# RMS norms at four stage boundaries: all eight blocks' squares summed by TensorE, and a weight split tied to the last residual

## The chip, the cores and the metric

The kernel runs on one core of one Trainium2 chip. The core's engines work from queues of their own: TensorE (PE; its weight loads are shown apart as PEld) multiplies matrices, VectorE (DVE) and ScalarE (ACT) do elementwise work, GpSimd (POOL) does next to nothing here, SyncE (SP) issues the transfers (DMAs). Each engine executes its own instructions strictly in the order in which they were recorded, and waits where an operand is not ready. The metric is the time of one execution in microseconds (us); of several runs the median is taken.

## The reference

The model is two blocks in a row on 256 tokens of width 1024, everything in float32. The first block has two layers, each a mixer (attention, short convolution, pooling) and a product-key expert layer ("peer"); the second block has another mixer, cross-attention and a gated feed-forward layer. Between the stages stands an RMS norm over the width of 1024:

```python
def rms_norm(t, g):
    tf = t.astype(jnp.float32)
    y = tf * lax.rsqrt(jnp.mean(tf * tf, axis=-1, keepdims=True) + EPS)
    return (y * g.astype(jnp.float32)).astype(t.dtype)

for l in range(DEPTH):                     # DEPTH = 2
    ...
    h = rms_norm(x, norm1_g[l]) * (1.0 + scale1) + shift1
    z = h @ w_in[l]
    ...
    x = x + gate1 * mix                    # mixer residual
    h2 = rms_norm(x, norm2_g[l]) * (1.0 + scale2) + shift2
    x = x + gate2 * peer_ffn(h2, peer_wq[l], ...)   # peer residual
# then the second block: h = rmsnorm(x, mix_norm_w); proj = h @ w_in_2; ...
```

## The kernel before

The activation `x` lies transposed in on-chip memory: eight blocks of 128 channels (partitions) by 256 tokens, `x[:, b]`. A float32 product is made from three products of rounded parts: every weight block of 128x1024 is loaded into a buffer `raw` (four of them), split by ScalarE into a high part `whi` (L509) and by VectorE into the rest `wlo` (L510), and multiplied by TensorE with the high and low parts `h` of the activation (L590, L591, L594; in the first two weight blocks behind a norm, whose matmuls are interleaved, L578, L579 and L582, below called the lead).

The method `norm` is called at four places, called boundaries here: from the first mixer to the first peer layer, from there to the second mixer, from there to the second peer layer, and from there to the mixer of the second block. It goes through these steps:

1. `warm(warm[0])`: 8 (before a peer layer) or 16 (before a mixer) warm-up matmuls (L546, a 128x512 product of the table `iota`, its result is read by nobody). `warm[1]` (6 or 8) and `warm[2]` (2 or 4) more follow below.
2. `rms_sums`: ScalarE squares each block into a tile `sq` (L471, out of a ring of four tiles of 128x256), as soon as that block's residual has been added (`use_out`, L894, in a mixer; `residual`, L1224, in a peer layer). For six blocks VectorE adds the squares up one after the other (L473); then TensorE multiplies that sum, and the squares of the last two blocks, with a column of ones (L465), two matmuls of one output column for each, and so adds over the channels into a tile of the PSUM pool C.
3. The split of the first weights behind the norm, tied by `issue_after(self.last_v)` to stand on VectorE behind the instruction that `last_v` names: the last of the five additions.
4. `rms_end`: mean and inverse root on VectorE (L479, L441 to L445), then TensorE spreads the row over the partitions (`rms_row`, L502), the second weights are split, and VectorE and ScalarE make `t`, `h` high and `h` low (L553, L561, L568) for the lead.

The order in each queue is made when the program is built: a scheduler places the instructions by their dependences and its own estimate of time, keeping to the order that `issue_after` asks for. So warm-up matmuls written behind the sums may land ahead of some of them. Other places of the program that sum squares (cross-attention, L1613, where TensorE takes all eight blocks; the feed-forward layer, L1675) do not go through `norm`.

Of the kernel before, what the change touches and what calls it, by code (L numbers as in the profile page):

```python
# [15 lines left out]
ALU = mybir.AluOpType  # L16
# [6 lines left out]
KB = 8  # L23
# [205 lines left out]
class Kernel:  # L229
# [287 lines left out]
    def norm(self, src, A, B=None, warm=WB):  # L517

        self.warm(warm[0])
        after = lambda: self.tc.issue_after(self.last_v)  # L520
        ss = self.rms_sums(src, KB)
        with after():
            a = self.split_w(self.next[0])
        with after():
            cols = self.rms_end(ss, D)
        self.warm(warm[1])
        row = self.rms_row(cols)
        self.warm(warm[2])
        with after():
            self.next = [a, self.split_w(self.next[1])]  # L530
        last = self.last_v
        pair = self.act_pair(self.wp, "h")
        t = {}
        for i in range(KB):
            with self.tc.issue_after(last):
                t[i] = self.norm_scale(src, A, row, i)
            self.norm_hi(pair, t[i], B, i)
        for i in range(KB):
            self.norm_lo(pair, t[i], B, i)
        return pair  # L540
# [153 lines left out]
    def mixer(self, l):  # L694
        nc, V, S, tc = self.nc, self.nc.vector, self.nc.scalar, self.tc
        with tc.tile_pool(name=f"att{l}", bufs=1) as ap:
# [194 lines left out]
            gate = self.mod[l][:, 16:24]  # L891

            def use_out(nb, ps):
                V.scalar_tensor_tensor(self.x[:, nb], ps, gate[:, nb:nb + 1], self.x[:, nb],  # L894
                                       op0=ALU.mult, op1=ALU.add)

            self.proj(self.a[f"wout{l}"], range(KB), (mhi, mlo), use_out,
                      kbs=[(k, k) for k in (4, 5, 6, 7, 0, 1, 2, 3)], each=each)
            each(99)
# [202 lines left out]
    def peer(self, l, keep, nxt, late=None):  # L1102
        nc, V, S, tc = self.nc, self.nc.vector, self.nc.scalar, self.tc
# [14 lines left out]
        with ExitStack() as st:  # L1118
# [69 lines left out]
            for i in range(NPEER):  # L1188
                vh, vl = self.split_w(self.raw(self.a[f"v{l}"][:, i]))
                src = gb[i // 64][:, i % 64]  # L1190
# [22 lines left out]
            gate = self.mod[l][:, 40:48]  # L1213
# [6 lines left out]
            def residual(b):  # L1220
                pt = self.pC([P, T])
                for t in range(2):
                    nc.tensor.transpose(pt[:, t * P:(t + 1) * P], yn[t][:, b * P:(b + 1) * P], self.ident)
                V.scalar_tensor_tensor(self.x[:, b], pt, gate[:, b:b + 1], self.x[:, b], op0=ALU.mult, op1=ALU.add)  # L1224

            for w in held:
                down(w, [0])
# [2 lines left out]
            for t in range(2):  # L1230
                residual(2 * t)
                residual(2 * t + 1)
                down(held[1], [1], [t])
            evacuate(1)
            for b in range(4, KB):
                residual(b)
# [544 lines left out]
```

## Time and profile before

| what | value |
|---|---|
| median of 3 runs | 2333.07 us (2330.46 to 2334.24) |
| the profiled execution, its whole time | 2334.84 us |
| its span (first to last instruction) | 2333.0 us |
| TensorE busy | 2297.4 us, 98% of the span |
| VectorE busy | 1904.7 us, 82% |
| ScalarE busy | 1208.7 us, 52% |
| mean granted clock of TensorE | 0.995 of full speed |
| share of TensorE in the chain that ended last | 91% (VectorE 5%, DMA 2%, ScalarE 1%) |

The span is what the rows further down divide up; 1.84 us of the execution lie outside it. The chain that ended last is followed back from the last instruction through what released each step; TensorE's share there says how much of the time is its own work. A line like "L546 A<-iota x8" is a group of like instructions of source line 546 that write a tile of the PSUM pool A from the tile `iota`. A matmul of float32 operands shows as two records in the trace, called passes below, so the two matmuls of one block's squares are four passes.

### The profile page before, as it was taken

How to read it: one execution, taken by the hardware profiler on the slowest of the kernel's cores; microseconds unless marked ns; L12 is line 12 of the kernel's file. 1: busy time of each engine (PE TensorE's matmuls, PEld its weight loads, DVE VectorE, ACT ScalarE, POOL GpSimd, SP SyncE). 2: the span in 40 equal slices, each digit the busy share in tenths (PEclk: the TensorE clock that was granted, in tenths of full speed). 3: DMA queues.
4: the chain of work that ended last, by engine and by line, in shares of the span. 5: the costliest groups of instructions: out<-in, count | busy, mean ns of one | idle time of the engine just before them, and what ended most of it. 6: DMA issues, size and time to landing. Idle time of an engine off the chain costs nothing.

```text
span 2333.0 us, 42534 instructions
## 1 busy us (share of the span) xinstructions
PE 2297.4 (98%) x16209; PEld 2046.3 (88%) x16209; DVE 1904.7 (82%) x4205; ACT 1208.7 (52%) x1884; POOL 4.8 (0%) x20
## 2 busy tenths in 40 slices
PE   8999999999999999999999999999999999999998
PEld 7989999988888878888999988888878878999997
DVE  6884999788899985576599888888888879767766
ACT  4474445555544455565454555554456654556553
POOL 0000000000000000000000000000000000000000
PEclk9999999999999999999999999999999999999999
DMA  8874556555677786544566655555556652345652
GB/s 300 284 259 156 200 198 214 177 171 172 224 228 235 256 297 201 175 141 130 172 207 200 204 173 171 171 173 176 172 183 193 193 181 84 123 165 189 194 187 82
DMA packets 124781, 443.96 MB, mean 190 GB/s; under 512 B 14240, under 2 KB 17440, under 8 KB 123808
## 3 DMA queue, kind: packets, MB, share of 16 engines
q1 hardware_dynamic: 124576, 441.24, 57.2%
q8 instruction: 127, 2.08, 0.4%
q14 instruction: 78, 0.64, 0.1%
HBM read 437.26 MB, written 3.93 MB: 189 GB/s over the span
## 4 chain that ended last, share of the span: by engine, by line
PE 91%; DVE 5%; DMA 2%; ACT 1%; issue 1%; SPq 0%; DVEq 0%; ACTq 0%
PE A L1183 29%; PE B L1140 10%; PE B L590 10%; PE B L591 10%; PE B L594 10%; PE B L1143 5%; PE A L1685 2%; PE C L1095 1%; PE C L1096 1%; DVE wlo L510 1%; PE C L594 1%; PE C L591 1%; PE C L590 1%; DMA adas<-in_wada 1%; PE A L935 1%
## 5 line engine op out<-in xcount | busy, mean ns | idle before, releaser
L510 DVE TENSOR_TENSOR wlo<-raw,whi 128x1024 fp32r<-128x1024 f32 (+1 forms) x715 | 849.0, 1189 | 249.2 <-issue 105.1
L509 ACT ACTIVATE whi<-raw 128x1024 fp32r<-128x1024 f32 (+1 forms) x715 | 735.7, 1032 | 219.0 <-PE B L594 126.9
L590 PE MATMUL B<-h,whi 128*128 128x256 f32 x2080 | 518.8, 286 | 0.6 <-ACT zs L1487 0.6
L591 PE MATMUL B<-h,whi 128*128 128x256 f32 x2080 | 515.7, 284 | 0.0
L590 PEld LDWEIGHTS B<-h,whi 128*128 128x128 f32 x2080 | 397.5, 191 | 3.5 <-ACT zs L1487 1.3
L591 PEld LDWEIGHTS B<-h,whi 128*128 128x128 f32 x2080 | 397.7, 191 | 2.3 <-issue 1.5
L1183 PE MATMUL A<-whi,ah 128*128 128x512 f32 x1024 | 323.1, 395 | 0.0
L1183 PE MATMUL A<-wlo,ah 128*128 128x512 f32 x1024 | 319.0, 392 | 2.4 <-DVE wlo L510 2.3
L1183 PE MATMUL A<-whi,al 128*128 128x512 f32 x1024 | 316.7, 389 | 0.0
L594 PE MATMUL B<-h,wlo 128*128 128x256 f32 x2080 | 293.9, 283 | 0.0
L509 ACT ACTIVATE ah<-gb 128x256 fp32r<-128x256 f32 x256 | 106.6, 417 | 323.1 <-PE A L1183 316.0
L594 PEld LDWEIGHTS B<-h,wlo 128*128 128x128 f32 x2080 | 268.5, 191 | 0.5 <-issue 0.3
L1140 PE MATMUL B<-h,whi 128*128 128x512 f32 x1024 | 260.8, 397 | 0.0
L1183 PEld LDWEIGHTS A<-wlo,ah 128*128 128x128 f32 x1024 | 191.7, 188 | 45.3 <-DVE wlo L510 5.1
L1183 PEld LDWEIGHTS A<-whi,al 128*128 128x128 f32 x1024 | 192.2, 188 | 41.9 <-DVE al L510 0.2
L1183 PEld LDWEIGHTS A<-whi,ah 128*128 128x128 f32 x1024 | 187.5, 188 | 34.9
L1140 PEld LDWEIGHTS B<-h,whi 128*128 128x128 f32 x1024 | 183.6, 189 | 32.2
L1143 PEld LDWEIGHTS B<-h,wlo 128*128 128x128 f32 x1024 | 139.7, 190 | 10.0
L1146 ACT ACTIVATE gb<-B 128x256 f32<-128x256 f32 x128 | 49.3, 385 | 187.5 <-PE B L1143 187.5
L1143 PE MATMUL B<-h,wlo 128*128 128x256 f32 x1024 | 142.5, 282 | 0.0
L510 DVE TENSOR_TENSOR al<-gb,ah 128x256 fp32r<-128x256 f32 x256 | 106.9, 417 | 0.0
L1130 ACT ACTIVATE gb<-B 128x512 f32<-128x512 f32 x64 | 38.4, 600 | 106.8 <-PE B L594 106.8
(483 smaller groups left out, 2805.1 us busy)
## 6 DMA issues: line engine op xcount, KB each, us to landing
raw<-in_u SPq DMA_DIRECT2D x256, 512.0 KB, 3.3
raw<-in_v SPq DMA_DIRECT2D x256, 512.0 KB, 4.2
raw<-in_win SPq DMA_DIRECT2D x50, 512.0 KB, 3.7
raw<-in_ffn SPq DMA_DIRECT2D x44, 512.0 KB, 4.2
adaw<-in_wada SPq DMA_DIRECT2D x40, 512.0 KB, 4.9
adas<-in_wada SPq DMA_DIRECT2D x40, 512.0 KB, 4.9
raw<-in_wq SPq DMA_DIRECT2D x32, 512.0 KB, 3.4
raw<-in_wout SPq DMA_DIRECT2D x24, 512.0 KB, 3.5
```

What stands on the lines that cost most here:

```text
L509: self.nc.scalar.activation(hi[s], src[s], AF.Copy)
L510: self.last_v = self.nc.vector.tensor_sub(lo[s], src[s], hi[s].bitcast(F32)).ins
L590: self.nc.tensor.matmul(ps, wh[:, s], xh[:, kx], start=first and i == 0, stop=False)
L591: self.nc.tensor.matmul(ps, wh[:, s], xl[:, kx], start=False, stop=False)
L594: self.nc.tensor.matmul(ps, wl[:, s], xh[:, kx], start=False, stop=last and i == n - 1)
L935: nc.tensor.matmul(sp[:, t, half], qs[2 * hd + half][:, t * P:(t + 1) * P], keys[:, half], start=True, stop=True)
L1130: S.activation(gb[i // 32][:, 2 * i:2 * i + 2], ps, AF.Gelu)
L1140: nc.tensor.matmul(ps, wh[:, k * P:(k + 1) * P], both[:, :, k], start=k == 0, stop=False, skip_group_check=True)
L1143: nc.tensor.matmul(ps[:, 0], wl[:, k * P:(k + 1) * P], h[0][:, k], start=False, stop=k == KB - 1, skip_group_check=True)
L1146: S.activation(gb[1][:, j + e], ps[:, 1], AF.Copy)
L1183: nc.tensor.matmul(y[t][c], a_[:, s], v_[:, c * 512:(c + 1) * 512], start=(i == 0 and n == 0), stop=(i == NPEER - 1 and n == 2), skip_grou ...
L1685: nc.tensor.matmul(y[t][c], x_[:, s], w_[:, c * 512:(c + 1) * 512], start=False, stop=j == FF - 1 and n == 2, skip_group_check=True)
```

## The change

`norm` asks `rms_sums` for all eight blocks on TensorE. With that the loop of additions has no block left, the sums go to a tile of the PSUM pool B instead of C (as `rms_sums` does wherever more than two blocks go to TensorE), and TensorE gets eight pairs of one-column matmuls at each boundary where it had three. Both residuals now note themselves in `last_v`; since no addition sets `last_v` any more, the split of the first weights is tied to stand behind the last residual.

```diff
@@ norm
-        ss = self.rms_sums(src, KB)
+        ss = self.rms_sums(src, KB, KB)
@@ mixer, use_out
-                V.scalar_tensor_tensor(self.x[:, nb], ps, gate[:, nb:nb + 1], self.x[:, nb],
-                                       op0=ALU.mult, op1=ALU.add)
+                self.last_v = V.scalar_tensor_tensor(self.x[:, nb], ps, gate[:, nb:nb + 1], self.x[:, nb],
+                                                     op0=ALU.mult, op1=ALU.add).ins
@@ peer, residual
-                V.scalar_tensor_tensor(self.x[:, b], pt, gate[:, b:b + 1], self.x[:, b], op0=ALU.mult, op1=ALU.add)
+                self.last_v = V.scalar_tensor_tensor(self.x[:, b], pt, gate[:, b:b + 1], self.x[:, b], op0=ALU.mult,
+                                                     op1=ALU.add).ins
```

First place: TensorE at the first boundary, from the last product of the first mixer (L594) to the row's spreading (L502). Before, eight warm-up matmuls stand ahead of the sums (the first of them is shown) and six behind (A_2138), then two more (A_2148):

```order
L594 MATMUL B_2044<-h_867,wlo_2041 128x256 x8
L414 MATMUL C_2075<-c1t,part_1853 128x1
L546 LDWEIGHTS iota
L546 MATMUL A_2083<-iota 128x512
...
L465 MATMUL C_2109<-c1t,sq_2106 128x1 x2
L465 MATMUL C_2109<-c1t,sq_2112 128x1 x2
L465 MATMUL C_2109<-c1t,sq_2116 128x1 x2
...
L546 MATMUL A_2138<-iota 128x512
...
L546 MATMUL A_2148<-iota 128x512
L502 MATMUL C_2145<-c1t,rs_2126 128x128 x2
```

And now; the same eight stand ahead, and the six of A_2143 stand two behind sq_2105, two behind sq_2109, one behind sq_2113 and one behind sq_2117 (only the first is shown):

```order
L546 MATMUL A_2083<-iota 128x512
...
L465 MATMUL B_2092<-c1t,sq_2093 128x1 x2
L465 MATMUL B_2092<-c1t,sq_2097 128x1 x2
L465 MATMUL B_2092<-c1t,sq_2101 128x1 x2
L465 MATMUL B_2092<-c1t,sq_2105 128x1 x2
...
L546 MATMUL A_2143<-iota 128x512
L465 MATMUL B_2092<-c1t,sq_2109 128x1 x2
...
L465 MATMUL B_2092<-c1t,sq_2113 128x1 x2
...
L465 MATMUL B_2092<-c1t,sq_2117 128x1 x2
...
L465 MATMUL B_2092<-c1t,sq_2121 128x1 x2
...
L546 MATMUL A_2153<-iota 128x512
...
L502 MATMUL C_2150<-c1t,rs_2131 128x128 x2
```

Five pairs of sums are new, and six warm-up matmuls moved from behind the sums to among them; the third boundary has the same order.

Second place: VectorE at the first boundary, from the residual of the sixth block to the mean (`ms`); `sq` are the squares, `wlo_2121` and `wlo_2126` the low part of the first weights. Before:

```order
L894 SCALAR_TENSOR_TENSOR x<-B_1972,mod_68,x 128x256
L421 TENSOR_TENSOR mod_68<-mod_68,vt 128x1
L473 TENSOR_TENSOR sq_2094<-sq_2094,sq_2092 128x256
...
L473 TENSOR_TENSOR sq_2106<-sq_2106,sq_2103 128x256
L894 SCALAR_TENSOR_TENSOR x<-B_2008,mod_68,x 128x256
L510 TENSOR_TENSOR wlo_2121<-raw_2079,whi_2120 128x1024
L894 SCALAR_TENSOR_TENSOR x<-B_2044,mod_68,x 128x256
L415 TENSOR_TENSOR mod_68<-C_2075,vt 128x1
L951 COPY nat_2206<-iota 128x16
L433 SCALAR_TENSOR_TENSOR Acol<-mod_68,vt 128x8
L479 TENSOR_SCALAR ms_2124<-C_2109 128x2
```

And now:

```order
L894 SCALAR_TENSOR_TENSOR x<-B_1972,mod_68,x 128x256
L421 TENSOR_TENSOR mod_68<-mod_68,vt 128x1
L894 SCALAR_TENSOR_TENSOR x<-B_2008,mod_68,x 128x256
L894 SCALAR_TENSOR_TENSOR x<-B_2044,mod_68,x 128x256
L415 TENSOR_TENSOR mod_68<-C_2075,vt 128x1
L510 TENSOR_TENSOR wlo_2126<-raw_2079,whi_2125 128x1024
L433 SCALAR_TENSOR_TENSOR Acol<-mod_68,vt 128x8
L951 COPY nat_2211<-iota 128x16
L955 CAST first_2213<-fd_2214 128x16
L479 TENSOR_SCALAR ms_2129<-B_2092 128x2
```

The five additions are gone and the split moved from ahead of the last residual to behind it.

Third place: TensorE at the second boundary, from the first transposes of the peer layer's upper half (L1223, `yn` is the layer's result) to the sums. Before, the warm-up matmuls of A_11552 stand 1, 4, 4, 1 and 6 in the gaps:

```order
L1223 MATMUL C_11517<-c1t,yn_11471 128x128
...
L1223 MATMUL C_11521<-c1t,yn_11471 128x128
...
L1223 MATMUL C_11517<-c1t,yn_11472 128x128
L1223 MATMUL C_11521<-c1t,yn_11472 128x128
...
L1223 MATMUL C_11525<-c1t,yn_11471 128x128
L1223 MATMUL C_11525<-c1t,yn_11472 128x128
...
L1223 MATMUL C_11529<-c1t,yn_11471 128x128
L1223 MATMUL C_11529<-c1t,yn_11472 128x128
...
L546 MATMUL A_11552<-iota 128x512
L465 MATMUL C_11586<-c1t,sq_11583 128x1 x2
```

And now 1, 2, 3, 1 and 9 (A_11557):

```order
L1223 MATMUL C_11522<-c1t,yn_11476 128x128
...
L1223 MATMUL C_11526<-c1t,yn_11476 128x128
...
L1223 MATMUL C_11522<-c1t,yn_11477 128x128
L1223 MATMUL C_11526<-c1t,yn_11477 128x128
...
L1223 MATMUL C_11530<-c1t,yn_11476 128x128
L1223 MATMUL C_11530<-c1t,yn_11477 128x128
...
L1223 MATMUL C_11534<-c1t,yn_11476 128x128
L1223 MATMUL C_11534<-c1t,yn_11477 128x128
...
L546 MATMUL A_11557<-iota 128x512
L465 MATMUL B_11574<-c1t,sq_11575 128x1 x2
```

Three warm-up matmuls moved from ahead of the last transposes to behind them; the sums that follow have six more among them (2, 2, 1, 1) as at the first boundary, and the fourth boundary has the order of the second. On SyncE one load of the peer layer's query weights (the fifth block) moved behind the loads of `keys`, `first` and `crow`, at the first and the third boundary.

## Rows read from the trace of the kernel before

**Rows 1.** The page: busy time of each engine, share of the span, instructions

```profile
PE 2297.4 (98%) x16209; PEld 2046.3 (88%) x16209; DVE 1904.7 (82%) x4205; ACT 1208.7 (52%) x1884; POOL 4.8 (0%) x20
```

**Rows 2.** Windows: stretch, its length, busy us by engine, TensorE clock, DMA

```profile
1200.00:1900.00 700.00, 699.20 (x4718) 609.37 (x4717) 607.13 (x1327) 370.58 (x532) 0.00 (x0) 1.00 0.57 184
```

**Rows 3.** Timeline, TensorE, first boundary: start, us, what, idle before and releaser

```profile
173.96 1.89 PE L546 MATMUL A<-iota 128*128 128x512 f16 x8
175.69 1.40 PE L465 MATMUL C<-c1t,sq 128*128 128x1 f32 x12
176.94 1.89 PE L546 MATMUL A<-iota 128*128 128x512 f16 x8
179.30 0.71 PE L502 MATMUL C<-c1t,rs 128*128 128x128 f32 x4 [0.47 <-DVE rs L445]
181.37 0.58 PE L578 MATMUL C<-h,whi 128*128 128x256 f32 x1 [1.36 <-ACT h L561]
...
186.75 0.52 PE L582 MATMUL C<-h,whi 128*128 128x256 f32 x3
```

**Rows 4.** Timeline, VectorE, first boundary

```profile
169.41 2.47 DVE L473 TENSOR_TENSOR sq<-sq,sq 128x256 f32<-128x256 f32 x5
...
172.19 1.22 DVE L510 TENSOR_TENSOR wlo<-raw,whi 128x1024 fp32r<-128x1024 f32 x1
174.02 0.48 DVE L894 SCALAR_TENSOR_TENSOR x<-B,mod,x 128x256 f32<-128x256 f32 x1 [0.62 <-PE B L594]
...
177.12 0.16 DVE L479 TENSOR_SCALAR ms<-C 128x2 f32<-128x2 f32 x1 [2.34 <-PE C L465]
```

**Rows 5.** Timeline, TensorE, third boundary

```profile
1090.92 1.40 PE L465 MATMUL C<-c1t,sq 128*128 128x1 f32 x12
1092.18 1.89 PE L546 MATMUL A<-iota 128*128 128x512 f16 x8
...
1096.61 0.39 PE L578 MATMUL C<-h,whi 128*128 128x256 f32 x1 [1.30 <-ACT h L561]
...
1100.55 0.52 PE L582 MATMUL C<-h,whi 128*128 128x256 f32 x3
```

**Rows 6.** Timeline, TensorE, second boundary

```profile
993.76 0.38 PE L1223 MATMUL C<-c1t,yn 128*128 128x128 f32 x2
993.97 1.46 PE L546 MATMUL A<-iota 128*128 128x512 f16 x6
995.37 1.47 PE L465 MATMUL C<-c1t,sq 128*128 128x1 f32 x12
996.70 2.75 PE L546 MATMUL A<-iota 128*128 128x512 f16 x12
```

**Rows 7.** Timeline, VectorE, second boundary

```profile
991.19 0.68 DVE L1218 TENSOR_SCALAR yn<-A 128x512 f32<-128x512 f32 x1
```

**Rows 8.** Timeline, VectorE, fourth boundary

```profile
1902.56 0.68 DVE L1218 TENSOR_SCALAR yn<-A 128x512 f32<-128x512 f32 x1
...
1904.07 0.43 DVE L473 TENSOR_TENSOR sq<-sq,sq 128x256 f32<-128x256 f32 x1 [0.49 <-ACT sq L471]
```

**Rows 9.** Timeline, TensorE, fourth boundary

```profile
1905.65 1.46 PE L546 MATMUL A<-iota 128*128 128x512 f16 x6
...
1908.45 2.75 PE L546 MATMUL A<-iota 128*128 128x512 f16 x12
```

**Rows 10.** Timeline, ScalarE, first boundary

```profile
174.54 0.42 ACT L471 ACTIVATE sq<-x 128x256 f32<-128x256 f32 x1 [1.81 <-DVE x L894]
```

**Rows 11.** Windows, the lead of the first boundary (columns as in rows 2)

```profile
181.30:184.70 3.40, 3.33 (x15) 3.33 (x16) 3.40 (x10) 2.74 (x8) 0.00 (x0) 0.50 0.48 154
```

**Rows 12.** Windows in cross-attention, from its own sums of squares on (columns as in rows 2)

```profile
2059.10:2062.00 2.90, 2.90 (x27) 2.86 (x26) 2.59 (x5) 2.09 (x6) 0.00 (x0) 1.00 0.00 0
2062.00:2064.30 2.30, 2.30 (x11) 2.30 (x12) 0.22 (x2) 2.07 (x3) 0.00 (x0) 0.51 0.69 228
2064.30:2068.80 4.50, 4.50 (x22) 4.50 (x22) 3.24 (x10) 0.00 (x0) 0.00 (x0) 0.50 0.29 102
```

## The prediction

> **What bounds the kernel now.** I read the page first: the reader is to see that TensorE is busy 98% of the span and VectorE 82% [rows 1]. Then the windows: over 700 us of peer layers and mixer TensorE is busy 699.2 us at full clock [rows 2], so whatever delays TensorE at one place is not made up behind it; a microsecond lost at a boundary is a microsecond of the kernel. Then the timelines of the four boundaries, TensorE beside VectorE, to see which wait ends last there. At the first boundary TensorE does not wait for VectorE's additions: they end at 171.88, the split of the first weights follows at 172.19, and then VectorE itself waits 0.62 us for TensorE's last product before the last residual, at 174.02 [rows 4]. TensorE meanwhile runs eight warm-up matmuls from 173.96, and the twelve passes of the sums from 175.69, without a gap [rows 3]; the last square, started at 174.54 and 0.42 us long [rows 10], had been ready for 0.7 us. The mean starts at 177.12, released by TensorE's sums after 2.34 us of VectorE's idleness [rows 4]. So the path from last residual to mean is TensorE's queue: 1.73 us of warm-up and 1.25 us of passes. Behind the mean nothing fills TensorE but the remaining eight warm-ups; it idles 0.47 us before the row and 1.36 us before the lead [rows 3].
>
> **The change, the first and the third boundary.** It takes five additions off VectorE, 2.47 us [rows 4], where they cost nothing: VectorE waits behind them anyway. It adds five pairs of sums, so 20 passes, on TensorE, on the path. A pass is (176.94 - 175.69) / 12 = 0.104 us [rows 3], at the third boundary (1092.18 - 1090.92) / 12 = 0.105 [rows 5]: 2.08 and 2.10 us. And the order puts six warm-up matmuls among the sums that stood behind them; one is (175.69 - 173.96) / 8 = 0.216 us [rows 3], so 1.30 us more before the mean. They gave work to time in which TensorE had to wait for the mean's chain; that time is idle now. Sum: 3.38 us at the first boundary, 3.40 at the third.
>
> **The second and the fourth boundary.** Here the squares wait for the residuals, these for transposes, and additions stand between the residuals. Before, the last transposes are over at 993.97 [rows 6]. Now seven warm-ups instead of ten stand ahead of them, and no addition. The limit is VectorE's copy of the layer's last quarter, which ends at 991.19 + 0.68 = 991.87 [rows 7]; with 0.08 us for the handover (an estimate), two transposes of 0.22, three warm-ups of 0.65, two transposes, one warm-up and two transposes of 0.22 each (993.97 - 993.76 is such a 0.21 [rows 6]) they end at about 993.54, 0.43 us earlier. At the fourth boundary ScalarE's split had delayed an addition, and the residuals behind it, by 0.49 us [rows 8]; the same count from 1902.56 + 0.68 gives 1904.85 for 1905.65 [rows 9], 0.80 earlier. From there on, before: six warm-ups and twelve passes, 996.70 - 993.97 = 2.73 us, and 1908.45 - 1905.65 = 2.80. Now: nine warm-ups (1.94), 32 passes of (996.70 - 995.37) / 12 = 0.111 [rows 6] (3.55) and six warm-ups among them (1.30), 6.79 us. So 6.79 - 2.73 - 0.43 = 3.63 at the second and 6.79 - 2.80 - 0.80 = 3.19 at the fourth. The four boundaries together: 3.38 + 3.63 + 3.40 + 3.19 = 13.6 us.
>
> **What I cost at nothing.** The first split now starts about 174.5 at the first boundary; it has 1.22 us [rows 4] and its product is not wanted before the lead at 181.37 [rows 3], and the mean, which is queued behind it on VectorE, comes after 180. Without that cover it would cost its 1.22 us. At the second and fourth boundary it stood behind the last residual already. The query weights' fifth load waits for the buffer that the first split frees, some 2.3 us later than before (the residual's end for 172.19), and now stands behind three other loads on SyncE; it is needed two weight blocks after the lead, behind 186.75 [rows 3]. If that cover were short the price would be a part of those 2.3 us, twice. The tile in pool B instead of C delays nobody: the mean reads it long before the third product wants it. The ring of four squares is a new wait: the fifth square can start only when TensorE has summed the first, since additions no longer free it. Its ScalarE time of 0.42 us [rows 10] lies beside TensorE's next three pairs and two warm-ups, 3 x 0.42 + 0.43 = 1.7 us, and ScalarE has queued only splits behind it. So nothing as long as the warm-ups stand there.
>
> **The clock.** The chip has two levels here, 2.4 GHz and 1.2 GHz (granted 1.00 and 0.50). At the first boundary it fell to 0.50 from 181.3 to 184.7, after the row's matmuls and the idle pieces [rows 11, 3]; the third boundary, with the same gaps, kept it. Price: from lead to xl-products 186.75 - 181.37 = 5.38 us against 1100.55 - 1096.61 = 3.94 [rows 3, 5], 1.44 us. In cross-attention there are rows for what the change adds: there TensorE sums eight blocks by these passes, and though it was busy 2.90 of 2.90 us the clock fell at 2062 and stayed at 0.50 until 2068.8 [rows 12]. At most half of those 6.8 us is lost, 3.4. Now every boundary has 4.6 to 4.9 us of such passes thinned by six warm-ups, then 0.43 to 1.3 us of warm-up, then the idle pieces. I expect a stretch of low clock at all four. Bounds for one: 0 (third boundary as it was) to 3.4 us; I take 2.1, nearer to 1.44, since part of the stretch is idle time or passes that slow by less than half. The first boundary pays its 1.44 already: 4 x 2.1 - 1.44 = 7.0 us.
>
> The Trainium skill bears on this in TensorE: Matmul & The Clock Gate, section Why this matters for your kernels: it warns of gaps without work between bursts of matmuls as what lowers the clock. By that the passes, which leave no gap, would cost no clock, and the sum would be 13.6 us. The rows of cross-attention speak against it: there the fall came with TensorE busy throughout.
>
> **Sum.** 13.6 + 7.0 = 20.6 us. Against the profiled execution (span 2333.0, 2334.84 with what lies outside) that is 2355.4; it stands 1.77 above the median of the runs, 2333.07, and on that I put it: 2353.7 us, 0.9% slower. A measurement here tells about 0.2%, or 4.7 us, from no change.
>
> **Rivals.** *The clock holds.* The six warm-ups among the sums and those before and behind keep the clock up as at the third boundary, and only the first boundary pays its 1.44 as before. For it: three of four boundaries kept it; against it: rows 12. It gives 2333.07 + 13.6 = 2346.7; without the first boundary's fall too, 2345.2. (This is also where the skill's rule leads.) *The ring of squares decides.* If handovers make every late pair wait for a square that waits for TensorE, each of the 16 late pairs takes 0.42 for the pair, 0.42 for the square and some 0.2 of handovers (an estimate), 1.0 instead of 0.75 with its warm-ups: 4 us more, 2357.7. It decides from the point where a square and its handovers take longer than the 1.7 us of cover; they don't by these rows. *Not slower.* The passes would have to fall in time that TensorE spends waiting anyway. Then only the residuals count: 0.43 and 0.80 us earlier, and the 0.27 us that the sums waited for the last square at those two boundaries (2.73 + 2.80 less twice six warm-ups and twelve passes, 2 x 2.63), 1.5 us: 2331.6. It decides if TensorE is idle before the mean for as long as the passes take; the rows show no such idleness ahead of the mean, only behind it. That the change doesn't do what it says can be excluded: additions are gone and pairs stand in the recorded order.
>
> **How the numbers follow.** Forecast 0.72, the clock holds 0.17, the ring 0.06, not slower 0.05. The time is the forecast's, 2353.7. The range reaches down to the clock's holding everywhere, 2345, and up past the ring to nearly four full prices of the clock (13.6 + 4 x 3.4 - 1.44 = 25.8 gives 2358.8; all four at once are unlikely): 2345 to 2358. It leaves out the not-slower case and the tops of the others, some 0.15. Slower by over 0.2% takes the first three, 0.95; of the rest 0.04 is within 0.2% and 0.01 faster.
>
> **What would show it.** Right: at the first and third boundary 16 passes, then six warm-ups among 16 more, about 4.8 us from first sum to mean where it was 1.4; ScalarE's squares five to eight released by TensorE; an idle piece of some 1.8 us before the row where it was 0.47; windows of 0.50 clock at all four boundaries. Wrong: sums that start before the first eight warm-ups, passes much shorter than 0.104, a full clock through every lead (the second case), late pairs that wait for ScalarE (the third), or work of the peer layers that catches up and gives the delay back.

## The result, and the profile after

| what | before | changed |
|---|---|---|
| median, runs side by side | 2331.32 us (2329.75 to 2334.24, 6 runs) | 2349.47 us (2346.15 to 2351.34, 6 runs) |
| ratio | 1 | 1.0073 (95%: 1.0062 to 1.0084) |
| the profiled execution, its span | 2333.0 us | 2347.7 us |

The change makes the kernel 0.73% slower, by the ratio 17.0 us (14.5 to 19.6; the two medians lie 18.2 us apart). Forecast were 20.6 us, and the time lies inside the range of 2345 to 2358 us. The page of the changed kernel, busy time of each engine as in [rows 1]:

```profile
PE 2309.4 (98%) x16289; PEld 2058.2 (88%) x16289; DVE 1897.9 (81%) x4185; ACT 1208.6 (51%) x1884; POOL 4.8 (0%) x20
```

VectorE lost 6.8 us of work, TensorE gained 12.0 us in 80 more records, which are the 20 passes at each of four boundaries, and the span grew by 14.7. The timeline of TensorE at the first boundary (start, us, what; in brackets the idle time before and who ended it) answers to [rows 3]:

```profile
171.38 1.89 PE L546 MATMUL A<-iota 128*128 128x512 f16 x8
173.10 1.84 PE L465 MATMUL B<-c1t,sq 128*128 128x1 f32 x16
174.80 0.59 PE L546 MATMUL A<-iota 128*128 128x512 f16 x2
175.23 0.50 PE L465 MATMUL B<-c1t,sq 128*128 128x1 f32 x4
175.59 0.59 PE L546 MATMUL A<-iota 128*128 128x512 f16 x2
...
177.18 0.50 PE L465 MATMUL B<-c1t,sq 128*128 128x1 f32 x4
177.54 0.59 PE L546 MATMUL A<-iota 128*128 128x512 f16 x2
179.90 0.71 PE L502 MATMUL C<-c1t,rs 128*128 128x128 f32 x4 [1.77 <-DVE rs L445]
181.97 0.39 PE L578 MATMUL C<-h,whi 128*128 128x256 f32 x1 [1.36 <-ACT h L561]
...
187.40 0.52 PE L582 MATMUL C<-h,whi 128*128 128x256 f32 x3
```

The reader sees the recorded order at work: 16 passes, then four late pairs with six warm-ups among them, and only two warm-ups left for the time in which the mean is made. TensorE's idle piece before the row is 1.77 us where it was 0.47 [rows 3]. VectorE at the same place, for [rows 4]:

```profile
171.44 0.48 DVE L894 SCALAR_TENSOR_TENSOR x<-B,mod,x 128x256 f32<-128x256 f32 x1 [2.31 <-PE B L594]
...
171.90 1.22 DVE L510 TENSOR_TENSOR wlo<-raw,whi 128x1024 fp32r<-128x1024 f32 x1
...
177.71 0.16 DVE L479 TENSOR_SCALAR ms<-B 128x2 f32<-128x2 f32 x1 [3.78 <-PE B L465]
```

The additions are gone; in their place VectorE waits longer for the last product (2.31 us for 0.62) and longer for the sums (3.78 for 2.34). From the residual to the mean it is 177.71 - 171.44 = 6.27 us where it was 177.12 - 174.02 = 3.10 [rows 4]: 3.17 us later. ScalarE's squares at the first boundary:

```profile
173.64 1.81 ACT L471 ACTIVATE sq<-x 128x256 f32<-128x256 f32 x4 [0.67 <-PE B L465]
```

Squares five to eight now wait for TensorE, as the ring of four makes them; but the last one is done at 173.64 + 1.81 = 175.45, and its pair starts at 177.18, behind the warm-ups. TensorE at the second and then at the fourth boundary, from the first transpose of the upper half on, answering to [rows 6, 9]:

```profile
993.07 0.27 PE L1223 MATMUL C<-c1t,yn 128*128 128x128 f32 x1
...
997.57 1.84 PE L465 MATMUL B<-c1t,sq 128*128 128x1 f32 x16
...
1001.73 0.85 PE L465 MATMUL B<-c1t,sq 128*128 128x1 f32 x4
1002.43 2.69 PE L546 MATMUL A<-iota 128*128 128x512 f16 x6
...
1010.80 0.52 PE L582 MATMUL C<-h,whi 128*128 128x256 f32 x3
...
1913.94 0.27 PE L1223 MATMUL C<-c1t,yn 128*128 128x128 f32 x1
...
1918.45 1.84 PE L465 MATMUL B<-c1t,sq 128*128 128x1 f32 x16
...
1922.53 0.50 PE L465 MATMUL B<-c1t,sq 128*128 128x1 f32 x4
1922.89 1.46 PE L546 MATMUL A<-iota 128*128 128x512 f16 x6
...
1931.16 0.52 PE L582 MATMUL C<-h,whi 128*128 128x256 f32 x3
```

The same transposes and first L582 products in the kernel before, which [rows 6, 9] do not show:

```profile
990.94 0.27 PE L1223 MATMUL C<-c1t,yn 128*128 128x128 f32 x1
...
1005.06 0.52 PE L582 MATMUL C<-h,whi 128*128 128x256 f32 x3
...
1902.21 0.27 PE L1223 MATMUL C<-c1t,yn 128*128 128x128 f32 x1
...
1916.73 0.64 PE L582 MATMUL C<-h,whi 128*128 128x256 f32 x4
```

And the third boundary of the changed kernel, answering to [rows 5]:

```profile
1096.65 1.84 PE L465 MATMUL B<-c1t,sq 128*128 128x1 f32 x16
...
1106.43 0.58 PE L578 MATMUL C<-h,whi 128*128 128x256 f32 x1 [1.19 <-ACT h L561]
...
1112.27 0.52 PE L582 MATMUL C<-h,whi 128*128 128x256 f32 x3
```

From these starts, the way through each boundary:

| boundary | from, to | before | changed | more |
|---|---|---|---|---|
| first | first warm-up, first L582 | 12.79 us | 16.02 us | 3.2 |
| second | first upper transpose, first L582 | 14.12 | 17.73 | 3.6 |
| third | first sum, first L582 | 9.63 | 15.62 | 6.0 |
| fourth | first upper transpose, first L582 | 14.52 | 17.22 | 2.7 |

Together 15.5 us, where the span grew by 14.7. Three more differences make up the rest: the first boundary is reached 2.6 us earlier (173.96 before, 171.38 now), the way from there to the second takes 1.5 us longer (990.94 - 186.75 = 804.19 before, 993.07 - 187.40 = 805.67 now), and 0.3 us lie behind the fourth. The first two differ between executions of one kernel: in a second profiled execution of the changed kernel they are 171.17 and 803.73. The clock at the boundaries (windows of the changed kernel; columns as in [rows 2], the clock is the number behind the POOL column):

```profile
182.40:185.70 3.30, 3.30 (x18) 3.30 (x17) 3.30 (x10) 2.23 (x6) 0.00 (x0) 0.50 0.39 142
993.10:1001.50 8.40, 8.40 (x59) 6.02 (x58) 3.62 (x6) 5.42 (x9) 0.00 (x0) 1.00 0.70 252
1001.50:1005.00 3.50, 3.50 (x13) 1.71 (x13) 2.04 (x12) 0.00 (x0) 0.00 (x0) 0.51 0.04 12
1100.50:1110.70 10.20, 7.58 (x33) 6.31 (x33) 8.26 (x26) 3.22 (x8) 0.00 (x0) 0.50 0.17 56
1927.00:1931.00 4.00, 3.77 (x31) 3.77 (x32) 4.00 (x12) 2.88 (x8) 0.00 (x0) 1.00 0.36 131
```

In this execution it fell to its lower level at the first boundary (in the lead, as before), at the second (from the last pair of sums to the row), for 10.2 us at the third, and not at the fourth. The second profiled execution of the same kernel (the repetition further down) shows it low at all four: in the lead of the first as here, and at the other three in these windows:

```profile
1004.30:1007.70 3.40, 3.40 (x16) 3.40 (x17) 3.40 (x10) 2.63 (x7) 0.00 (x0) 0.50 0.47 155
1103.30:1110.10 6.80, 5.67 (x26) 5.67 (x27) 6.43 (x17) 3.23 (x8) 0.00 (x0) 0.50 0.24 80
1925.90:1929.30 3.40, 3.40 (x16) 3.40 (x17) 3.40 (x10) 2.56 (x7) 0.00 (x0) 0.50 0.45 153
```

The ways through the four boundaries, counted as in the table but from the first warm-up at the third, are 16.00, 18.81, 17.03 and 18.72 us there.

### The profile page after: what moved, and what is told of

The parts are those of the page before. It is cut to its first block, busy times and chain, and to the rows that moved or that the text cites. A ratio compares the mean times of both kernels' runs of the same rounds, so it can differ in the third digit from the quotient of the medians.

```text
span 2347.7 us, 42682 instructions
## 1 busy us (share of the span) xinstructions
PE 2309.4 (98%) x16289; PEld 2058.2 (88%) x16289; DVE 1897.9 (81%) x4185; ACT 1208.6 (51%) x1884; POOL 4.8 (0%) x20
## 3 DMA queue, kind: packets, MB, share of 16 engines
HBM read 437.26 MB, written 3.93 MB: 188 GB/s over the span
## 4 chain that ended last, share of the span: by engine, by line
PE 91%; DVE 4%; DMA 2%; issue 1%; ACT 1%; SPq 0%; DVEq 0%; ACTq 0%
PE A L1183 28%; PE B L1140 10%; PE B L590 10%; PE B L594 10%; PE B L591 10%; PE B L1143 5%; PE A L1686 2%; PE C L1095 1%; PE C L1096 1%; DMA adas<-in_wada 1%; DVE wlo L510 1%; PE A L627 1%; PE B L465 1%; PE A L546 1%; PE C L594 1%
## 5 line engine op out<-in xcount | busy, mean ns | idle before, releaser
L594 PE MATMUL B<-h,wlo 128*128 128x256 f32 x2080 | 293.9, 283 | 0.0
L594 PEld LDWEIGHTS B<-h,wlo 128*128 128x128 f32 x2080 | 268.5, 191 | 0.5 <-issue 0.3
```

Of the source, the lines that this page charges most:

```text
L594: self.nc.tensor.matmul(ps, wl[:, s], xh[:, kx], start=False, stop=last and i == n - 1)
```

## The experiments

Two theories. *Queue*: the loss is TensorE's passes and the warm-ups that came among them, 13.6 us; the clock adds little. *Clock*: it adds 7.0 us, about a third of the whole. Beside them, that the split's new place or the lack of additions costs or gives something of its own.

**The split's place alone.** The kernel before with its additions, the split of the first weights tied to the last residual:

```diff
@@ norm (and last_r noted in both residuals)
-        with after():
+        with self.tc.issue_after(self.last_r):
             a = self.split_w(self.next[0])
```

> The kernel before, with one part of the change alone: the split of the first weights is tied to the last residual, the additions and the three pairs of sums stay. Theory of TensorE's queue (the added passes and the warm-ups that moved among them lie on the path, all else is covered): the split has more than 4 us until the lead wants it; the only thing moved on TensorE is one warm-up among the sums at the first and third boundary, 2 x 0.216 = +0.4 us, ratio 1.000. Rival, the split's place costs: its 1.22 us delays the mean or the lead at the two to four boundaries, +2.4 to +4.9 us, ratio 1.001 to 1.002.

Measured: 2332.21 us beside 2331.95, ratio 1.0004 (0.9995 to 1.0013). No cost shows; the interval allows up to 3 us, so of the rival's 2.4 to 4.9 us the upper part is excluded.

**The additions alone left out.** The kernel before without the five additions at the boundaries, so that the sums lack five blocks:

```diff
@@ norm
-        ss = self.rms_sums(src, KB)
+        ss = self.rms_sums(src, KB, add=False)
```

> The kernel before with the five additions left out at each boundary, so that only the last three blocks' squares are summed (the squares of the first five are made and not used); three pairs of sums as before. Queue theory: at the first and third boundary nothing changes, since VectorE waited behind the additions; at the second and fourth the order has nine warm-ups instead of six behind the last transposes, as in the changed kernel, and the transposes come 0.4 to 0.8 us earlier: 3.27 - 2.73 - 0.43 = +0.1 and 3.27 - 2.80 - 0.80 = -0.3 us, ratio 1.000. Rival, the additions were on the path: up to 2.1 to 2.5 us less at each boundary, -5 to -10 us, ratio 0.996 to 0.998, and then the changed kernel's loss would be larger still than its passes.

Measured: 2331.67 beside 2331.95, ratio 0.9995 (0.9986 to 1.0004). With no addition to stand behind, the split of the first weights also moved here, ahead of the last two residuals of the first boundary. The additions were off the path: taking them away bought at most 3.3 us by the interval, and nothing that shows, so nothing offsets what TensorE pays.

**The warm-ups behind the sums.** The changed kernel with the second warm-ups tied behind the last sum:

```diff
@@ norm (last_s is the last matmul of square_sums)
-        self.warm(warm[1])
+        with self.tc.issue_after(self.last_s):
+            self.warm(warm[1])
```

> The changed kernel with the second group of warm-ups tied behind the last sum, so that the 32 passes of a boundary stand in one piece and the six warm-ups fill the wait for the mean's chain again. Queue theory: 4 x 6 x 0.216 = 5.2 us of the loss go, about +12 us over the kernel before, ratio 1.005. Rival, the clock makes most of the loss: the six warm-ups among the passes then help it, and without them it falls earlier in all four boundaries; no gain, +17 to +20 us, ratio 1.007 to 1.009.

Measured: 2342.86 beside 2331.95, ratio 1.0048 (1.0035 to 1.0062), 11.2 us slower than before. TensorE at its first boundary:

```profile
171.84 3.63 PE L465 MATMUL B<-c1t,sq 128*128 128x1 f32 x32
175.33 1.89 PE L547 MATMUL A<-iota 128*128 128x512 f16 x8
177.69 0.71 PE L502 MATMUL C<-c1t,rs 128*128 128x128 f32 x4 [0.47 <-DVE rs L445]
```

The 32 passes take 175.33 - 171.84 = 3.49 us where twelve took 1.25 [rows 3]; the idle piece before the row is 0.47 again. Against the changed kernel's 1.0073, and 1.0069 in its repetition below, that is 4.9 to 5.8 us less, with some 4 us either way; the prediction had put 4 x 1.30 = 5.2 us of warm-ups on the path. By the rows it is a little less: from first sum to row 179.90 - 173.10 = 6.80 us became 177.69 - 171.84 = 5.85, so 0.95 us at this boundary. The passes get longer when they stand in one piece, 3.49 / 32 = 0.109 us, which takes back a part of the 1.30.

**Idle time filled.** The changed kernel with six more warm-ups ahead of the row, run twice, the second time beside the unaltered changed kernel:

```diff
@@ norm
-        self.warm(warm[2])
+        self.warm(warm[2] + 6)
```

> The changed kernel with six more warm-ups in the last group, recorded behind the last sum and ahead of the row at each boundary, where TensorE idles 1.0 to 1.8 us in the changed kernel. Nothing that the path needs waits for them as long as they end before the row (8 x 0.216 = 1.73 us). Queue theory: no change against the changed kernel, +17 us, ratio 1.007. Rival, the clock: with the idle piece filled it stays up in some of the leads, 1.4 to 5 us less, +12 to +15.6 us, ratio 1.005 to 1.0065.

> The changed kernel once more, beside the filled one on one chip. Both theories: +17 us over the kernel before, ratio 1.006 to 1.008. Its profile is a further look at the clock: by the theory that low stretches come and go with no fixed place, they lie elsewhere than in the first profile (3.4 us at the first and second boundary, 10.2 us at the third, none at the fourth); by the theory that each boundary has a fixed price, the same.

> The changed kernel with six more warm-ups ahead of the row, once more, beside the changed kernel on one chip. Clock theory: less low clock than the changed kernel in the four boundaries and 2 to 4 us less time, ratio 1.005 to 1.006. Theory that only passes and warm-ups on the path count: the same time as the changed kernel, within 0.5 us.

Measured: filled 2345.96, ratio 1.0059 (1.0045 to 1.0073), and again 2344.31, ratio 1.0054 (1.0041 to 1.0067); the changed kernel itself beside it 2347.14, ratio 1.0069 (1.0056 to 1.0082). All runs of the second filled kernel (2343.58 to 2346.22) lie below all of the changed one (2346.70 to 2349.72). TensorE of the first filled one, first boundary:

```profile
177.35 1.89 PE L546 MATMUL A<-iota 128*128 128x512 f16 x8
179.71 0.71 PE L502 MATMUL C<-c1t,rs 128*128 128x128 f32 x4 [0.47 <-DVE rs L445]
```

The warm-ups lie in time in which TensorE waited, so the queue is as long as before, and still some 3 us go. That is the clock's part, as far as this filling gives it back; it is about half of 7.0. The profiled executions agree: the low stretches at the four boundaries make some 17 us in each of the two of the changed kernel, and 6.8 and 10.2 us in those of the two filled ones. Whether the gain belongs to the change is asked further down. Of the two theories that the repetition was to part, that of low stretches with no fixed place holds: in its profile they lie elsewhere in part, and at the fourth boundary too.

**Six pairs instead of eight.**

```diff
@@ norm
-        ss = self.rms_sums(src, KB, KB)
+        ss = self.rms_sums(src, KB, 5)
```

> The changed kernel with five blocks' squares on TensorE alone and the first three added up on VectorE: six pairs of sums at a boundary in place of eight. Queue theory: 12 passes more than before, and four warm-ups among the sums: at the first and third boundary 12 x 0.104 + 4 x 0.216 = 2.1 us; at the second and fourth three to four warm-ups more stand ahead of the last transposes (0.65 to 0.86), then two, 24 passes and four: 0.43 + 2.66 + 0.86 - 2.73 = 1.2, with the 0.65 to 0.86 about 2.0. In all +8.2 us, with some of the clock's price up to +11, ratio 1.0035 to 1.0047. Rival, a threshold (a wait that comes with the pool or the tied split, whatever the count): as the changed kernel, 1.007.

Measured: 2341.05 beside 2331.43, ratio 1.0043 (1.0030 to 1.0056). In the same comparison three pairs stand at 0, six at 10.0 us and eight at 16.1: 3.3 us for each of the first three pairs more, 3.0 for each of the last two, over four boundaries. The cost grows with the passes and the warm-ups that come among them; the 1.007 of a threshold lies outside the interval.

**One pair.** The other way: the kernel before with all eight blocks added on VectorE, and three of the warm-ups before a peer layer moved behind its sums:

```diff
-WB = (8, 6, 2)
+WB = (5, 9, 2)
@@ rms_sums (the only pair is then also the last)
-            self.square_sums(ss, prev, True, False)
+            self.square_sums(ss, prev, True, npe == 0)
@@ norm
-        ss = self.rms_sums(src, KB)
+        ss = self.rms_sums(src, KB, 0)
```

> The other way: from the kernel before, all eight blocks added up on VectorE, one pair of sums on TensorE, and the first group of warm-ups before a peer layer cut from 8 to 5 with the second raised from 6 to 9. Queue theory: eight passes (0.84 to 0.89 us) and at the first and third boundary one warm-up (0.22) less ahead of the mean, while the last addition (0.42) comes in behind the last square, covered by warm-ups: -1.05 us at the first and third boundary, -0.1 to -0.4 at the second and fourth, -2.4 us in all, ratio 0.999, below what a few runs tell surely. Rival, two more additions on VectorE cost what TensorE saves: 1.000.

Measured: 2334.15 beside 2331.43, ratio 1.0011 (1.0001 to 1.0020): the gain did not come. VectorE and then TensorE at its second boundary:

```profile
994.71 1.47 DVE L473 TENSOR_TENSOR sq<-sq,sq 128x256 f32<-128x256 f32 x3
996.10 1.22 DVE L510 TENSOR_TENSOR wlo<-raw,whi 128x1024 fp32r<-128x1024 f32 x1
997.24 0.15 DVE L479 TENSOR_SCALAR ms<-C 128x2 f32<-128x2 f32 x1
```

```profile
996.33 0.58 PE L465 MATMUL C<-c1t,sq 128*128 128x1 f32 x4 [0.58 <-DVE sq L473]
996.77 1.89 PE L546 MATMUL A<-iota 128*128 128x512 f16 x8
```

TensorE now waits 0.58 us for the last addition, and the split, which is tied to that addition, stands between it and the mean: the sums are over about 996.77, the mean starts at 997.24, when VectorE is free. So the last VectorE instructions had become the path there: the way through the second and fourth boundary, from the first upper transpose to the lead's last products, takes 15.01 and 15.18 us (14.12 and 14.52 before), while the third, from the first warm-up, takes 10.81 for 11.37. This is read from the rows; a version with the split elsewhere was not run.

**Filling both kernels.** The control for the filled kernels above: the kernel before with five warm-ups behind the row's matmuls, and the changed kernel with these five and the six ahead of the row.

```diff
@@ norm (last_b is the last matmul of bcast_cols; the "+ 6" in the changed kernel only)
-        self.warm(warm[2])
+        self.warm(warm[2] + 6)
+        with self.tc.issue_after(self.last_b):
+            self.warm(5)
```

> The kernel before, with five more warm-up matmuls recorded behind the row's two matmuls, where TensorE waits 1.24 to 1.36 us for the lead's h; five of them take 1.08 us, so the queue pays nothing. A control: does filling idle time speed up this kernel in general? If the 3 us that the filling gave back in the changed kernel belong to the change, this one gains at most the 1.44 us of the first boundary's low clock: ratio 0.9994 to 1.0000. If filling gains anywhere, whatever the sums do: 0.9987 or less. If the matmuls delay the lead: above 1.0005.

> The changed kernel with six more warm-up matmuls ahead of the row and five behind it, so that of TensorE's idle time at a boundary some 0.8 us are left. The queue's share alone is 13.6 us, ratio 1.0058 (by the changed kernel's rows, with late pairs of 0.37 instead of 0.42 us, some 13: 1.0056). If the filling ahead of the row has given back all that the clock took: 1.0054 to 1.0059, as without the five behind. If the clock still falls at boundaries for the idle time behind the row: 1.0045 to 1.005.

Measured: the kernel before, filled, 2331.50 beside 2333.03, ratio 0.9991 (0.9983 to 1.0000); the changed one, filled at both places, 2345.01, ratio 1.0055 (1.0042 to 1.0068). TensorE of the filled kernel before at its first boundary, and a window of the lead behind it, for [rows 3, 11]:

```profile
177.83 1.24 PE L548 MATMUL A<-iota 128*128 128x512 f16 x5
179.36 0.39 PE L580 MATMUL C<-h,whi 128*128 128x256 f32 x1 [0.29 <-ACT h L563]
```

```profile
179.30:183.30 4.00, 3.94 (x33) 3.94 (x34) 4.00 (x11) 2.72 (x8) 0.00 (x0) 1.00 0.41 131
```

The lead runs at full clock there, and the kernel before gains some 2.1 us too (0 to 4.0). So filling is not a cure of what the change did alone; the measured value lies between the two expectations for this control and the interval reaches into both, so they are not parted. With both kernels filled, the change costs 1.0055 - 0.9991 = 0.0064, 15 us with some 3.6 either way (by the medians 13.5): the queue's 13.6 with little or no clock in it. The rows of the two say it more closely, since both run at full clock through all four boundaries. The third boundary, first in the kernel before, filled, and then in the changed one, filled at both places, with a window of the latter:

```profile
1086.19 1.90 PE L548 MATMUL A<-iota 128*128 128x512 f16 x8
...
1097.56 0.52 PE L584 MATMUL C<-h,whi 128*128 128x256 f32 x3
```

```profile
1093.61 1.90 PE L548 MATMUL A<-iota 128*128 128x512 f16 x8
...
1108.15 0.52 PE L584 MATMUL C<-h,whi 128*128 128x256 f32 x3
```

```profile
1093.60:1108.20 14.60, 13.82 (x98) 10.57 (x97) 9.77 (x29) 5.83 (x13) 0.00 (x0) 1.00 0.34 119
```

From first warm-up to the lead's last products (L584 here, L582 before) it is 11.37 us and 14.54, 3.17 more. The four boundaries, counted so or from the first upper transpose, take 11.34, 14.12, 11.37 and 14.67 us and 14.53, 17.46, 14.54 and 17.47: the queue alone costs 3.19, 3.34, 3.17 and 2.80, together 12.5 us. In time, five more warm-ups behind the row gave the changed kernel nothing that shows beyond the six ahead of it.

**Fewer warm-ups ahead of the sums.** The filled kernel before, and three of its eight warm-ups before a peer layer moved behind the sums:

```diff
-WB = (8, 6, 2)
+WB = (5, 9, 2)
```

> The kernel before with five warm-up matmuls instead of eight ahead of the sums at the first and third boundary (the three go behind them), and five behind the row. There the eight, 1.73 us, stand between the last product and the sums, while the last square is ready 0.7 us before the sums. If the queue ahead of the sums is the path, each of these two boundaries gains 0.65 us, together 1.3, ratio 0.9994, less what the first boundary's clock gives: 0.9988 to 0.9994. If the last square is late then, or the clock falls for want of the three: 1.0000 or above.

Measured: 2329.83 beside 2333.03, ratio 0.9989 (0.9979 to 0.9998). It is below both kernels of this case, by 0.1% only. Its TensorE at the first boundary:

```profile
173.72 1.24 PE L548 MATMUL A<-iota 128*128 128x512 f16 x5
174.79 1.40 PE L465 MATMUL C<-c1t,sq 128*128 128x1 f32 x12
```

Five warm-ups take 1.07 us where eight took 1.73 [rows 3], and the sums still follow without a wait. That is the 0.65 us that the expectation had for this boundary. The step from the filled kernel (0.9991) to this one is 0.5 us by the ratios and 1.7 by the medians, expected were 1.3; the intervals hold all of these.

## Why the prediction was right, and where not

**The bound.** Right. What delayed TensorE at a boundary was not made up behind it: the ways between the boundaries take 804.2, 85.9 and 801.7 us before and 805.7, 85.9 and 801.7 after the change. Additions and split, costed at nothing, cost nothing that the runs show (0.9995 and 1.0004, each with some 2 us either way).

**The queue, 13.6 us.** Right in place and nearly in size: 12.5 us at full clock, from the two filled kernels. At the first boundary, where the clock's price is the same in both (from lead to first L582 5.43 us, before 5.38 [rows 3]), 3.2 us came for 3.38. At the fourth, at full clock, 2.7 for 3.19. At the second 3.6 came for 3.63, but 0.4 of it is the clock's: the sums took 1002.43 - 997.57 = 4.86 us where those of the fourth took 1922.89 - 1918.45 = 4.44. The small miss is the late pairs: the step took the 0.104 to 0.111 us of a pass in a row of twelve, and a late pair between warm-ups took 175.59 - 175.23 = 0.36 us, 0.09 for a pass. The two parts of 3.38 were shown apart when the warm-ups went behind the sums: the 20 passes cost 3.49 - 1.25 = 2.24 us for 2.08, the warm-ups 0.95 for 1.30. The count at the second boundary has a slip: the terms that give 1904.85 at the fourth give 993.48, not 993.54. Its 0.08 us for the handover came from no row; in the changed kernel the transposes start 0.05 us behind the copy's end, at 994.01 behind 993.27 + 0.69.

**The clock, 7.0 us.** Mis-sized: the extra over the queue's 12.5 us was 3.0 us in the first profiled execution of the changed kernel and 5.3 in the second. "At all four" failed in the first, which had no low stretch at the fourth boundary, and came in the second. A stretch was priced at 2.1 us; one of 3.4 us inside a lead cost 1.4 to 1.5 (the leads of the second and fourth boundary took 3.93 us in the first execution and 5.44 and 5.43 in the second). At the third, the 10.2 us of the first execution cost 5.99 - 3.17 = 2.8, of which 1112.27 - 1106.43 = 5.84 us from lead to first L582 for 3.94 [rows 5] make 1.9; the second boundary's stretch in that execution lay mostly beside the mean's chain and cost 0.4. By the runs, 17.0 and 16.1 us less 12.5 leave 3.6 to 4.5, and less the 13.5 to 15 of the filled kernels 1 to 3.5, each with some 3 us or more either way. The step erred in the price of a stretch, and in taking the one that the kernel before had in its one profile as a property of a place: of three profiled executions with three pairs of sums and no fillers (the kernel before, the split moved, the additions left out) all had it at the first boundary, and two at the third, which in the prediction had "kept it".

The Trainium skill, TensorE: Matmul & The Clock Gate, section Part 1: The HAM clock gate (the "warmup" mystery), says of sustained work at the start of a kernel that the point at which the clock changes varies from one run to the next. Here two executions of one kernel differ in low stretches in its middle; whether for the same reason, no run here shows.

**The rivals.** The clock's holding (2346.7) was as near as the forecast: 13.6 us more were its sum, 20.6 the forecast's, 17.0 came. Queue and clock were both priced too high, so the time came between the two sums and does not part them by itself. What parts them are the profiles, with low stretches at three boundaries in one execution and at four in the other, and the mean granted clock of the runs: 0.9953 to 0.9962 in the three comparisons of the kernel before, 0.9927 and 0.9932 in the two of the changed one. The ring of squares did become a wait, as the step on it said, and was covered by the warm-ups among the sums. With them behind the sums the ring stands without that cover, and that kernel still needed 3.49 us for 32 passes, so TensorE hardly waited there either. "Not slower" fell: no idle time lay ahead of the mean.

**Signs named ahead.** The idle piece of some 1.8 us before the row came (1.77). The 4.8 us from first sum to mean came as 177.71 - 173.10 = 4.61. The clock at 0.50 at all four boundaries came in one of the two profiled executions.

## What to carry to other kernels

Where TensorE is busy throughout, work moved to it from an engine that has slack costs its full price, and an addition that lies beside TensorE's work is free as long as TensorE's own queue ends later: five at a boundary were, of seven the last ones became the path at two of the four. Filler matmuls are free only behind the last instruction that the waiting engine needs: a change of what stands in the queue can move them onto the path, so look where each one lands in the recorded order. Price a possible fall of the clock as a chance with a size, not as a fixed cost of a place seen once.

## What the runs showed of the hardware

The stretches at half clock move between executions of one kernel. In the changed kernel's first profiled execution they made some 3.4, 3.5 and 10.2 us at the first three boundaries, in the second 3.4, 3.4, 6.8 and 3.4 at all four (windows above). One of 3.4 us inside a lead, which takes 3.9 us at full clock, cost 1.4 to 1.5 us.

They were absent where TensorE's wait ahead of the lead was filled. Of the three kernels with five warm-ups behind the row, one profiled execution each, none had a low stretch at any of its four boundaries; of the ten profiled executions without them (the experiments' among them) 22 of 40 boundaries had one. These are few executions, most of them of different kernels, so it is a count and not a test. Over all runs the mean granted clock was 0.9927 and 0.9932 in the changed kernel, 0.9950 and 0.9948 with six warm-ups more ahead of the row, 0.9956 with five behind it as well, and 0.9953 in the kernel before beside that last one.

A busy TensorE does not exclude the fall: in the changed kernel's first execution the clock fell at 1001.5, at the second boundary, after TensorE had by the profile been busy 8.40 of 8.40 us (window 993.10 to 1001.50 above), in warm-ups, transposes and one-column passes. What makes it fall at one boundary and not at another with the same instructions stays open.
